# GpSimd makes the low parts of two of three weight chunks in the mixing stages of a two-block layer stack

## Chip, cores and metric

One core of one Trainium2 chip runs the whole program. The time is device microseconds of one execution; what is compared is the median of several runs. Three runs of the kernel before took 1978.05, 1983.33 and 1986.85 us.

## What is computed

The input is one sequence of 512 tokens of width 1024 and a context of 256 tokens. A first block of two layers (windowed attention, a Fourier mix, a short convolution, gated merge) gives x; a second block of two layers follows. A layer of the second block, cut to what matters here:

```python
def hybrid_layer(x, ...):
    proj = x @ w_in                                   # 1024 -> 2336
    o_a = dilated_mixture(...)                        # 6 heads
    o_b = rms_norm(diff_attention(...), subln_g)      # 4 heads, two softmaxes each
    q = rms_norm(c_q, q_norm_g) @ w_uq
    kv = rms_norm(c_kv, kv_norm_g) @ w_ukv
    o_c = causal_attention(...)                       # 6 heads
    h = layer_norm(ALPHA * x + concat(o_a, o_b, o_c) @ w_o, ...)
    ffn = (silu(h @ w_gate) * (h @ w_up)) @ w_down
    return layer_norm(ALPHA * h + ffn, ...)
```

All of it is float32, with a result close to float32 precision.

## The kernel before

**Split numbers.** Every matrix product is made of three TensorE products. A float32 operand is split into a high part (ScalarE writes a copy in TensorE's shorter float type, `hi`, L165) and a low part (VectorE subtracts the high part from the original, `lo`, L169, or L171 with a scale). `mm3` (L212 to L214) then adds high by high, high by low and low by high in one PSUM bank. A weight chunk goes through `w` (from L178): SyncE's queue loads it into a raw tile `wr` (3 buffers), ScalarE writes `wh`, VectorE writes `wl` from `wr` and `wh`, both of which lie in SBUF. There are 5 buffers each of `wh` and `wl`, and 2 more that a chunk takes when its running number modulo 7 is 2 or 5. A full chunk is 128 partitions by 1024 elements; 299 chunks pass through `w`.

**A layer of the second block** is a mixing stage (`second_mix`) and an output stage (`second_out`: w_o, the gated feed-forward product, two layer norms). A mixing stage uses 22 chunks: four of 128x832 for the latent projection (`proj_nat`, token tile by token tile), fifteen of 128x1024 for `proj_t` (three for each of five units of the kinds A and B), two of 128x768 for w_uq and one for w_ukv. There are eight units of two heads each, in the order B, C, B, C, A, C, A, A. A unit's projections are written ahead of the attention of the unit before it, and the attention stands at a higher priority; a list scheduler of the tile framework sets the order on each engine from dependencies, priorities and its own estimates. That order is fixed when the program is built, and each engine takes its instructions strictly one after another.

**Unit B** (`differential`): the projection lies in PSUM, and for each of four tiles ScalarE writes the high part (L165) and VectorE the low part (L171 for queries, L169 for keys), in turn; then GpSimd copies the high part to a third place (L1163, `qk<-qk`), and only then can the scores (L1025, `sps<-qk`) be made. Attention itself (`att2`): VectorE adds the bias table and takes the minimum (L1028), ScalarE takes the exponential (L1032), TensorE turns tiles (L1058), ScalarE and VectorE split them (`pth`, `ptl`), TensorE multiplies by V (L1074, L1075).

**GpSimd's queue before** holds: the reciprocal root of every norm (`rstd`: `rv` L219, `rr` L222), the loads of the bias tables (L950, which wait for a table's buffer), the copies L1163 and L1135, the zeroing L1133 and L1160, and loads and stores of activations (L897, L907, L1343). At the seam of the two blocks the last norm of the first block runs for token tiles 0 to 3: `rv` and `rr` on GpSimd, the scaling of x on VectorE (L905, two instructions a tile), a store (L907), then TensorE's transposes `tps<-ident,x` (L410), which feed the latent projection.

Of the kernel before, what the change touches and what calls it, by code (L numbers as in the profile page):

```python
# [9 lines left out]
F32 = mybir.dt.float32  # L10
F32R = mybir.dt.float32r
AF = mybir.ActivationFunctionType
ALU = mybir.AluOpType
# [27 lines left out]
def _host_constants():  # L41
# [27 lines left out]
    def dft(n):  # L69
        k = np.arange(n)  # L70
        w = 2.0 * np.pi * ((k[:, None] * k[None, :]) % n) / n
        return np.cos(w) / math.sqrt(n), np.sin(w) / math.sqrt(n)
# [45 lines left out]
class _Kernel:  # L118
    def __init__(self, es, tc, A, out):
        self.tc, self.nc, self.A, self.out = tc, tc.nc, A, out  # L120
        E = es.enter_context
        self.wx, self.wi = None, 0
        self.cst = E(tc.tile_pool(name="cst", bufs=1))
        self.sm = E(tc.tile_pool(name="sm", bufs=8))
        self.wp = E(tc.tile_pool(name="wp", bufs=5))
        self.xp = E(tc.tile_pool(name="xp", bufs=1))
        self.ps = E(tc.tile_pool(name="ps", bufs=1, space=PSUM))
        self.dr = E(tc.tile_pool(name="dr", bufs=1, space=DRAM))
        self.fp_es = ExitStack()
        self.fp = self.fp_es.enter_context(tc.tile_pool(name="fp", bufs=1, reuse_waits="tile"))  # L130
# [48 lines left out]
    def w(self, shape, parts, post=None):  # L179

        raw = self.wp.tile([P] + shape, F32, tag="wr", bufs=3, name="wr")
        for dst, src in parts:
            self.nc.sync.dma_start(raw if dst is None else dst(raw), src)
        if post is not None:
            post(raw)
        self.wi += 1
        if self.wx is not None and self.wi % 7 in (2, 5):
            pool, x, n = self.wx, "x", 2
        else:
            pool, x, n = self.wp, "", 5  # L190
        h = pool.tile([P] + shape, F32R, tag="wh" + x, bufs=n, name="wh")
        l = pool.tile([P] + shape, F32R, tag="wl" + x, bufs=n, name="wl")
        self.split(h, l, raw)
        return h, l

    def wblock(self, src, c0, n=P):
# [758 lines left out]
    def second(self):  # L955
        tc, nc, A = self.tc, self.nc, self.A
        with ExitStack() as es:
            self.sp = es.enter_context(tc.tile_pool(name="sp", bufs=1, reuse_waits="tile"))
            self.wx = self.sp
            self.rope2 = self.sp.tile([P, SEQ], F32, name="rope2")  # L960
            nc.gpsimd.dma_start(self.rope2, A["rope2"])
            self.ropek = self.sp.tile([P, NX, 64], F32, name="ropek")
            nc.gpsimd.dma_start(self.ropek, A["ropek"])
            self.half2 = self.sp.tile([P, 2], F32, name="half2")
            nc.gpsimd.memset(self.half2, 0.0)
            nc.gpsimd.memset(self.half2[0:64, 0:1], 1.0)
            nc.gpsimd.memset(self.half2[64:128, 1:2], 1.0)
            for l in range(DEPTH):
                with tc.tile_pool(name="a2", bufs=2, reuse_waits="tile") as pool:
                    heads = self.second_mix(l, pool)  # L970
                with tc.tile_pool(name="o2", bufs=2, reuse_waits="tile") as pool:
                    self.second_out(l, pool, heads)

# [357 lines left out]
    def second_out(self, l, pool, heads):  # L1331
# [71 lines left out]
        for gi, nf in enumerate(groups):  # L1403
# [20 lines left out]
            def down(t, c, w):  # L1424
                tok = slice(t * P, (t + 1) * P)
                ps = self.acc(c.stop - c.start)
                self.mm3(ps, [(Hs[k][0][:, tok], Hs[k][1][:, tok]) + w(k) for k in range(nf)])
                h = H[t]
                nc.vector.scalar_tensor_tensor(  # L1429
                    h[:, c], h[:, c], ALPHA if gi == 0 else 1.0, ps, op0=ALU.mult, op1=ALU.add  # L1430
                )
# [76 lines left out]
```

## Time and profile before

| what | value |
|---|---|
| median of 3 runs | 1983.33 us (1978.05 to 1986.85) |
| profiled execution | 1981.64 us |
| its span, first to last instruction | 1979.9 us |
| mean granted TensorE clock | 0.993 of 2.4 GHz |
| TensorE (PE) busy | 1901.3 us, 96% |
| VectorE (DVE) busy | 1203.6 us, 61% |
| ScalarE (ACT) busy | 894.1 us, 45% |
| GpSimd (POOL) busy | 169.7 us, 9% |

The profiled execution is 1.7 us below the median, and 1.7 us of it lie outside the span. Busy shares are means over stages; the rows below show them by stage. A line number such as L169 is that of the kernel before; where a helper does the work, all its uses have one line and the tile's name tells them apart.

### The profile page before, as it was taken

The page shows a single profiled execution, that of the slowest core. Times are in us where ns is not written, and L with a number is a line of the kernel's source. Part 1 is how long each engine was busy: PE and PEld are TensorE (multiplying, and loading weights), DVE is VectorE, ACT ScalarE, POOL GpSimd, SP SyncE. Part 2 cuts the span into 40 slices and gives each one's busy share as a digit, 9 for nine tenths or more (in the row PEclk, how much of TensorE's full clock was granted, in tenths as well). Part 3 has the DMA queues.
Part 4 walks back from the last instruction along what each step waited for, and adds up shares of the span by engine and source line. Part 5 has one row for each costly group of instructions (what it writes and reads, how often), then busy time and mean ns, then how long its engine had stood idle before and what let it go on. Part 6 is the DMA issues. An engine that isn't in the chain of part 4 may idle for free.

```text
span 1979.9 us, 25710 instructions
## 1 busy us (share of the span) xinstructions
PE 1901.3 (96%) x9564; PEld 1560.8 (79%) x9564; DVE 1203.6 (61%) x2350; ACT 894.1 (45%) x1744; POOL 169.7 (9%) x299
## 2 busy tenths in 40 slices
PE   6999999999999999899999999999999999999997
PEld 3878788778878777777888888887777788888886
DVE  3759984375988578776733434366876664243444
ACT  4736662384755558665221322215866432132220
POOL 2100000030000132101200000012211010000001
PEclk9999999999999999999999999999999999999999
DMA  8414342042332361223432324325122332232421
GB/s 291 148 54 140 96 128 85 23 160 79 118 87 63 111 167 43 65 86 111 119 96 85 107 75 117 94 80 130 41 64 95 124 107 96 75 117 64 128 75 43
DMA packets 220448, 197.19 MB, mean 100 GB/s; under 512 B 30154, under 2 KB 178128, under 8 KB 220324
## 3 DMA queue, kind: packets, MB, share of 16 engines
q1 hardware_dynamic: 209940, 160.32, 27.3%
q0 software_dynamic: 10384, 35.24, 5.2%
q8 instruction: 75, 1.23, 0.3%
q14 instruction: 49, 0.40, 0.1%
HBM read 187.09 MB, written 12.03 MB: 101 GB/s over the span
## 4 chain that ended last, share of the span: by engine, by line
PE 80%; ACT 6%; DVE 5%; issue 2%; DMA 1%; POOL 1%; POOLq 0%; DVEq 0%; ACTq 0%; SPq 0%
PE acc L212 22%; PE acc L213 22%; PE acc L214 22%; PE sps L1025 2%; PE tps L792 1%; PE tps L1058 1%; ACT wh L165 1%; PE pv L803 1%; PE pv L1074 1%; PE pv L804 1%; DVE wl L169 1%; PE pv L1075 1%; PE tps L410 1%; DMA wr<-in_w_mod_dram 1%; ACT L L1032 1%
## 5 line engine op out<-in xcount | busy, mean ns | idle before, releaser
L165 ACT ACTIVATE wh<-wr 128x1024 fp32r<-128x1024 f32 (+3 forms) x299 | 311.9, 1045 | 605.3 <-PE acc L213 262.5
L169 DVE TENSOR_TENSOR wl<-wr,wh 128x1024 fp32r<-128x1024 f32 (+3 forms) x299 | 358.3, 1202 | 259.2 <-ACT wh L165 256.5
L212 PE MATMUL acc<-xt,wh 128*128 128x512 f32 (+1 forms) x1200 | 465.9, 388 | 2.1 <-DVE kb L169 1.7
L214 PE MATMUL acc<-xt,wl 128*128 128x512 f32 (+1 forms) x1200 | 464.7, 387 | 0.0
L213 PE MATMUL acc<-xt,wh 128*128 128x512 f32 (+1 forms) x1200 | 463.7, 386 | 0.0
L212 PEld LDWEIGHTS acc<-xt,wh 128*128 128x128 f32 x1200 | 226.2, 188 | 41.5 <-DVE kb L169 2.4
L214 PEld LDWEIGHTS acc<-xt,wl 128*128 128x128 f32 x1200 | 226.1, 188 | 39.8
L213 PEld LDWEIGHTS acc<-xt,wh 128*128 128x128 f32 x1200 | 226.2, 188 | 39.2
L212 PE MATMUL acc<-wh,ht 128*128 128x512 f32 (+1 forms) x494 | 193.1, 391 | 1.3 <-ACT ht L165 1.1
L213 PE MATMUL acc<-wl,ht 128*128 128x512 f32 (+1 forms) x494 | 192.1, 389 | 0.0
L214 PE MATMUL acc<-wh,ht 128*128 128x512 f32 (+1 forms) x494 | 191.7, 388 | 0.0
L165 ACT ACTIVATE pth<-tps 128x384 fp32r<-128x384 f32 (+1 forms) x176 | 90.1, 536 | 90.4 <-PE tps L792 48.4
L169 DVE TENSOR_TENSOR ptl<-tps,pth 128x384 fp32r<-128x384 f32 (+1 forms) x176 | 104.7, 614 | 25.4 <-ACT pth L165 24.1
L212 PEld LDWEIGHTS acc<-wh,ht 128*128 128x128 f32 x494 | 92.9, 188 | 23.0 <-ACT ht L165 2.6
L214 PEld LDWEIGHTS acc<-wh,ht 128*128 128x128 f32 x494 | 93.0, 188 | 21.2 <-DVE ht L169 0.4
L213 PEld LDWEIGHTS acc<-wl,ht 128*128 128x128 f32 x494 | 92.9, 188 | 20.0
L1032 ACT ACTIVATE L<-L,nm 128x512 f32<-128x512 f32 (+3 forms) x160 | 89.0, 557 | 31.2 <-DVE nm L1028 29.8
L1429 DVE SCALAR_TENSOR_TENSOR h<-h,acc 128x512 f32<-128x512 f32 (+1 forms) x50 | 33.2, 665 | 114.9 <-PE acc L214 114.9
L1395 DVE SCALAR_TENSOR_TENSOR th<-th,acc 128x512 f32<-128x512 f32 x42 | 28.9, 688 | 113.3 <-PE acc L214 113.1
L1028 DVE CUSTOM_DVE_ANT_0 L<-sps,T 128x512 f32<-128x512 f32 (+3 forms) x160 | 75.4, 487 | 25.4 <-PE sps L1025 23.5
L219 POOL TENSOR_SCALAR rv<-bna 128x1 f32<-128x1 f32 x16 | 18.8, 1173 | 789.0 <-DVE bna L1324 789.0
L214 PE MATMUL acc<-wh,xt 128*128 128x256 f32 (+2 forms) x256 | 85.1, 333 | 1.0 <-DVE xt L169 0.8
(317 smaller groups left out, 3352.2 us busy)
## 6 DMA issues: line engine op xcount, KB each, us to landing
wr<-in_w_in_dram SPq DMA_DIRECT2D x66, 512.0 KB, 4.6
wr<-in_w_gate_dram SPq DMA_DIRECT2D x44, 512.0 KB, 3.8
wr<-in_w_up_dram SPq DMA_DIRECT2D x44, 512.0 KB, 3.9
wr<-in_w_down_dram SPq DMA_DIRECT2D x42, 512.0 KB, 3.5
wr<-in_w_mod_dram SPq DMA_DIRECT2D x40, 512.0 KB, 4.5
wr<-in_w_o_dram SPq DMA_DIRECT2D x32, 256.0 KB, 3.6
T<-skew POOLq DMA_DIRECT2D x26, 256.0 KB, 2.9
x<-in_x_dram POOLq DMA_DIRECT2D x8, 512.0 KB, 7.1
```

Of the source, the lines that this page charges most:

```text
L165: self.nc.scalar.activation(out, in_, AF.Copy, scale=scale)
L169: self.nc.vector.tensor_tensor(out, in_, hi.bitcast(F32), op=ALU.subtract)
L212: mm(ps, lh, rh, start=(first and i == 0), stop=False)
L213: mm(ps, lh, rl, start=False, stop=False)
L214: mm(ps, ll, rh, start=False, stop=(last and i == n - 1))
L410: nc.tensor.transpose(v[:, k, :], src[:, (kb * 4 + k) * P : (kb * 4 + k + 1) * P], self.ident)
L792: nc.tensor.transpose(tp[:, hq * P : (hq + 1) * P], Ps[hq][:, i * P : (i + 1) * P], self.ident)
L1025: nc.tensor.matmul(ps[:, :w], x[:, tok], y[:, :w], start=(k == 0), stop=(k == len(s) - 1))
L1028: nc.vector.tensor_tensor_reduce(lc, ps[:, :n], T[:, SEQ - n : SEQ], 1.0, 3.0e38, op0=ALU.add, op1=ALU.min, accum_out=nm[:, i : i + 1],)
L1032: nc.scalar.activation(lc, lc, AF.Exp, bias=nm[:, i : i + 1], scale=-1.0, accum_out=sums[:, i : i + 1])
L1395: nc.vector.scalar_tensor_tensor(th, th, 0.5, pu, op0=ALU.mult, op1=ALU.mult)
L1429: nc.vector.scalar_tensor_tensor(h[:, c], h[:, c], ALPHA if gi == 0 else 1.0, ps, op0=ALU.mult, op1=ALU.add)
```

## The change

A field `share` is 0, except while `second_mix` is written out, where it is 2. In `w`, a chunk whose running number modulo 3 is below `share` has its low part subtracted by GpSimd instead of VectorE; the high part stays on ScalarE.

```diff
         h = pool.tile([P] + shape, F32R, tag="wh" + x, bufs=n, name="wh")
         l = pool.tile([P] + shape, F32R, tag="wl" + x, bufs=n, name="wl")
-        self.split(h, l, raw)
+        self.hi(h, raw)
+        if self.wi % 3 < self.share:
+            self.nc.gpsimd.tensor_tensor(l, raw, h.bitcast(F32), op=ALU.subtract)
+        else:
+            self.lo(l, raw, h)
         return h, l
...
                 with tc.tile_pool(name="a2", bufs=2, reuse_waits="tile") as pool:
+                    self.share = 2
                     heads = self.second_mix(l, pool)
+                    self.share = 0
```

29 of the 44 chunks of the two stages move: 15 in the first (three of 128x832, ten of 128x1024, two of 128x768), 14 in the second (two, ten, two). The scheduler then sets a new order. Lines behind L193 are 6 higher in the changed kernel, and behind L970 8 higher.

**GpSimd, the seam of the blocks and the head of the first mixing stage.** `rv_7012` and `rr_7014` are the norm of token tile 3, the last of the first block. Before:

```order
L967 MEMSET half_7043 64x1
L907 DMA xs_6582<-x 128x1024
L219 TENSOR_SCALAR rv_7012<-ssum 128x1
L222 TENSOR_TENSOR rr_7014<-rv_7012,mhalf 128x1
L907 DMA xs_6582<-x 128x1024
L1100 DMA dl<-in_diff_lambda_dram 128x128
```

Now:

```order
L197 TENSOR_TENSOR wl<-wr,wh 128x832
L972 MEMSET half_7043 64x1
L973 MEMSET half_7043 64x1
L197 TENSOR_TENSOR wl<-wr,wh 128x832
L913 DMA xs_6582<-x 128x1024
L225 TENSOR_SCALAR rv_7012<-ssum 128x1
L228 TENSOR_TENSOR rr_7014<-rv_7012,mhalf 128x1
L197 TENSOR_TENSOR wl<-wr,wh 128x1024
L913 DMA xs_6582<-x 128x1024
L197 TENSOR_TENSOR wl<-wr,wh 128x1024
L1108 DMA dl<-in_diff_lambda_dram 128x128
```

Two low parts of 832 elements now stand ahead of the norm of tile 3, and two of 1024 behind it.

**GpSimd, the copies of the first unit B in the first mixing stage.** The eight copies are four for queries, then four for keys. Before:

```order
L222 TENSOR_TENSOR rr_7255<-rv_7253,mhalf 128x2
L1163 COPY qk<-qk 32x512 x2
L1160 MEMSET qk 32x512
L1163 COPY qk<-qk 32x512 x4
L1160 MEMSET qk 32x512
L1163 COPY qk<-qk 32x512 x2
L950 DMA T<-skew 128x512 x4
```

Now:

```order
L228 TENSOR_TENSOR rr_7255<-rv_7253,mhalf 128x2
L197 TENSOR_TENSOR wl<-wr,wh 128x1024
L1171 COPY qk<-qk 32x512 x2
L1168 MEMSET qk 32x512
L1171 COPY qk<-qk 32x512 x2
L197 TENSOR_TENSOR wl<-wr,wh 128x1024
L1171 COPY qk<-qk 32x512 x2
L1168 MEMSET qk 32x512
L1171 COPY qk<-qk 32x512 x2
L956 DMA T<-skew 128x512 x4
```

One low part stands ahead of the first query copy, another between the query copies and the key copies.

**TensorE, the first scores of that unit**, among the products of its V projection. Before:

```order
L213 MATMUL acc<-xt,wh 128x512
L214 MATMUL acc<-xt,wl 128x512
L212 MATMUL acc<-xt,wh 128x512
L1025 MATMUL sps<-qk 128x256
L213 MATMUL acc<-xt,wh 128x512
L214 MATMUL acc<-xt,wl 128x512
L212 MATMUL acc<-xt,wh 128x512
L213 MATMUL acc<-xt,wh 128x512
L214 MATMUL acc<-xt,wl 128x512
L1025 MATMUL sps<-qk 128x256
```

Now (the same stretch of the projection, from five products earlier):

```order
L219 MATMUL acc<-xt,wh 128x512
L1033 MATMUL sps<-qk 128x256
L220 MATMUL acc<-xt,wl 128x512
L218 MATMUL acc<-xt,wh 128x512
L219 MATMUL acc<-xt,wh 128x512
L220 MATMUL acc<-xt,wl 128x512
L218 MATMUL acc<-xt,wh 128x512
L1033 MATMUL sps<-qk 128x256
```

Both score products stand five products earlier than before.

## Rows read from the trace of the kernel before

**Rows 1.** Busy time by stage: microseconds, then PE, PEld, DVE, ACT, POOL, clock, DMA

```profile
702.00:913.00 211.00, 195.00 (x1013) 155.58 (x1012) 161.30 (x399) 143.19 (x345) 38.05 (x62) 0.99 0.28 79
915.00:1336.00 421.00, 420.51 (x1951) 348.65 (x1952) 193.94 (x237) 108.80 (x141) 19.73 (x25) 1.00 0.33 99
1340.00:1552.00 212.00, 195.96 (x1003) 155.66 (x1002) 159.24 (x397) 141.98 (x343) 37.13 (x60) 0.98 0.28 79
```

**Rows 2.** Waits of PE, 702 to 913 us: total us, times, longest us

```profile
PE acc L999 <- ACT vt L996: 4.1, 5, 1.4
PE tps L1118 <- DVE sq L1113: 2.4, 1, 2.4
PE sps L1025 <- DVE nm L1028: 1.5, 3, 0.6
PE tps L1058 <- DVE ptl L169: 1.4, 2, 1.3
PE acc L212 <- DVE V L1004: 1.0, 1, 1.0
PE pv L1074 <- DVE heads L1085: 0.9, 1, 0.9
PE tps L1272 <- DVE ct L171: 0.9, 1, 0.9
```

**Rows 3.** Low parts of weights on DVE, 702 to 853 us: ns min/median/max, shapes

```profile
L169 DVE TENSOR_TENSOR wl<-wr,wh x17: 947/1218/1226, 703.0 to 851.6; 128x1024 fp32r<-128x1024 f32 x14, 128x768 fp32r<-128x768 f32 x3
```

**Rows 4.** DVE in time: start us, us, what [idle before, releaser]

```profile
693.25 1.95 DVE L169 TENSOR_TENSOR wl<-wr,wh 128x832 fp32r<-128x832 f32 x2
696.99 1.41 DVE L905 SCALAR_TENSOR_TENSOR x<-y,rr,x 128x512 f32<-128x512 f32 x2
698.31 1.22 DVE L169 TENSOR_TENSOR wl<-wr,wh 128x1024 fp32r<-128x1024 f32 x1
...
721.09 1.23 DVE L169 TENSOR_TENSOR wl<-wr,wh 128x1024 fp32r<-128x1024 f32 x1 [0.80 <-ACT wh L165]
...
726.30 1.23 DVE L169 TENSOR_TENSOR wl<-wr,wh 128x1024 fp32r<-128x1024 f32 x1 [0.59 <-ACT wh L165]
```

**Rows 5.** POOL in time: tiny norms, copies, a table load

```profile
692.43 0.12 POOL L965 MEMSET half<- 128x2 f32 x1
...
695.45 0.19 POOL L219 TENSOR_SCALAR rv<-ssum 128x1 f32<-128x1 f32 x1 [1.27 <-DVE ssum L901]
...
721.68 1.11 POOL L1163 CAST qk<-qk 32x512 fp32r<-32x512 f32 x1 [5.43 <-ACT qk L165]
723.72 0.60 POOL L1163 CAST qk<-qk 32x512 fp32r<-32x512 f32 x1 [0.93 <-ACT qk L165]
...
759.28 0.79 POOL L1163 CAST qk<-qk 32x512 fp32r<-32x512 f32 x1 [3.48 <-ACT qk L165]
...
833.13 0.20 POOL L219 TENSOR_SCALAR rv<-ssb 128x8 f32<-128x8 f32 x1 [3.13 <-DVE ssb L1184]
```

**Rows 6.** PE in time: transposes at the seam, two first uses, scores, two waits

```profile
697.84 0.63 PE L410 MATMUL tps<-ident,x 128*128 128x128 f32 x4
...
698.93 0.44 PE L213 MATMUL acc<-wl,xt 128*128 128x416 f32 x1
...
714.67 0.39 PE L214 MATMUL acc<-xt,wl 128*128 128x512 f32 x1
...
729.11 0.36 PE L1025 MATMUL sps<-qk 96*128 96x256 f32 x1
...
733.66 0.66 PE L999 MATMUL acc<-ident,vt 128*128 128x128 f32 x4 [1.27 <-ACT vt L996]
735.20 1.31 PE L1272 MATMUL tps<-ident,xs 128*128 128x128 f32 x8 [0.89 <-DVE ct L171]
```

**Rows 7.** Costliest POOL arithmetic of 700 to 915 us, shapes apart: busy us, mean ns

```profile
L222 POOL TENSOR_TENSOR rr<-rv,mhalf 128x8 f32<-128x8 f32 x2 | 3.3, 1668 | 0.2
```

**Rows 8.** Busy time and clock around one group of waits in the second mixing stage

```profile
1368.00:1392.00 24.00, 19.87 (x89) 14.54 (x88) 18.89 (x51) 17.28 (x44) 2.90 (x5) 0.86 0.20 56
```

More of the change, by code (lines that the diff above doesn't have):

```diff
@@ L969, in second @@
                 with tc.tile_pool(name="a2", bufs=2, reuse_waits="tile") as pool:
+                    self.share = 2
                     heads = self.second_mix(l, pool)
+                    self.share = 0
                 with tc.tile_pool(name="o2", bufs=2, reuse_waits="tile") as pool:
```

## The prediction

> **What bounds the kernel now.** I read the busy time by stage first [rows 1]. In the output stage between the mixing stages TensorE is busy for 420.5 of 421 us: nothing on another engine can shorten it, and the change leaves it alone. The two mixing stages are different: TensorE is busy for 195.0 of 211 us and for 196.0 of 212 us, so 16 us stand idle in each, 32 us in all, or 1.6% of the time. That is the most that any relief of VectorE can bring. VectorE is the next busiest there (161 and 159 us, three quarters), GpSimd the least (38 and 37 us, under a fifth). The list of waits then says who ends TensorE's idle time [rows 2]: the six largest rows that name VectorE make 8.1 us, the one that names ScalarE (`vt`) 4.1 us. None names a weight's low part, so no product waits for weights; what a low part can do is stand ahead of something else on VectorE.
>
> That weights are early is seen from a low part and its first use: the one made at 698.31 [rows 4] is first read by TensorE at 714.67 [rows 6], 15 us after its end. It is the first of the fifteen full chunks, with the shortest lead of them, as the later ones are made up to seven buffers ahead. Only the 832 wide chunks at the seam are closer: the pair that ends at 695.2 [rows 4] is first read until 698.93 [rows 6], under 4 us later.
>
> **What leaves VectorE.** The median full low part takes 1.22 us and the 768 wide one 0.95 us [rows 3]; two of 832 take 1.95 us together [rows 4]. The 29 that move are 20 x 1.22 + 4 x 0.95 + 5 x 0.98 = 33.1 us, about 16.5 us in each stage, a tenth of VectorE's work there.
>
> **What arrives on GpSimd.** The trace has no large two-input subtraction on GpSimd. The nearest row is a copy of 512 elements at 0.60 us [rows 5], 1.2 ns an element with one input. From below, two inputs cost no more than one: 1.2 us for 1024. From above, twice the price of reading both in turn: 4.8 us. I take the middle, both inputs read in turn, 2.4 us for 1024, 1.95 us for 832. The `rr` row would give far more (1.67 us for 8 elements [rows 7]), but that one raises to a power; the copy is a plain pass like the subtraction, so I hold it nearest. By the Trainium skill (GPSIMD Engine Reference, section 3.1) a tensor-tensor addition of 2048 elements takes 4.5 us, so an estimate of 2.25 us for 1024; the sum would move by some tenths. At 2.4 us the 29 take 20 x 2.4 + 4 x 1.8 + 5 x 1.95 = 65 us, and GpSimd's busy time rises from 38 to some 71 of 211 us: still no bound as an engine. What counts is the queue, as each low part waits for its high part and everything behind it waits too.
>
> **Place one, the seam, a loss.** Tile 3's norm starts on GpSimd at 695.45, after 1.27 us of idle time [rows 5]. The scaling on VectorE (696.99) follows and, with no time to spare, TensorE's transposes at 697.84 [rows 4, 6], between products that are ready. Now two 832 wide low parts stand ahead of that norm. The first can begin when the memset of 692.43 is over, near 692.6, and VectorE's work on tile 2 may hold it to 693.3. Two times 1.95 us end near 697.2; still ahead of their products (698.93); with the store behind them the norm starts 1.9 us late or a little more. VectorE has lost the same two low parts and is waiting then, so the 1.9 us reach the transposes whole: **+1.9 us**. Other products are ready by then, but TensorE takes its queue in order and stands at the transposes. In the second mixing stage the new order has the 832 wide parts a tile earlier, behind the store of tile 2: nothing, or at worst 1.9 us again.
>
> **Place two, the first unit B, a gain.** The eight splits run in turn over ScalarE and VectorE; low parts at 721.09 and 726.30 [rows 4] each delay that chain by up to 1.2 us, and behind it stand `vt` (wait 1.27 us at 733.66) and `ct` (0.89 us at 735.20) [rows 6]. In the first stage both of those low parts move, and the next one, beside `ct`, stays. Against that, the copy of the first key tile now stands behind a low part which cannot start before its high part (VectorE waited for that one until 726.30 [rows 4]; I add 0.3 us, as ScalarE now makes a fourth query split ahead of it) and ends near 729.0; the copy follows until 729.6. The scores that need it stood at 729.11 and are now five products earlier, near 728.0: a new wait of about 1.5 us where 0.5 us was. But TensorE waits behind this for `vt` and `ct` anyway, so the group ends when their chain does. The chain is 2.4 us shorter and gets some of that back as `vt` now follows the next chunk's high part; I take **-0.7 us** for the group in the first stage. In the second stage the low part beside `ct` moves too and no low part stands between the copies: **-1.8 us**. There the clock is 0.86 over 24 us [rows 8], that is part of the time at the lower level, after the same group of waits; in the first stage it is not. What this costs, 24 x 0.14 = 3.4 us, may come back or may befall the first stage; I count neither and keep it for the range.
>
> **Everything else.** Some 6 us of VectorE-ended waits remain in each stage; a tenth less work there is worth 0.6 us a stage. I set this against VectorE being held up by GpSimd's reads (below) and count zero. Lateness of low parts I cost at nothing: the 15 us above cover a low part of 2.4 us that waits behind a table load. If one took 15 us more, the products themselves would wait next.
>
> **Sum:** 1.9 - 0.7 - 1.8 = -0.6 us against the profiled 1981.64 us, which is 1.7 us below the median of the runs shown. As a median I expect 1983.33 - 0.6 = **1982.7 us**: no change. Runs of one kernel spread over 0.45%, so 0.5%, 9.9 us, is about what a measurement can tell here.
>
> **Rival one: the queue costs more than it gives (slower).** A low part takes 4.8 us instead of 2.4. Each place where a short GpSimd step stands closely behind one then overruns its idle time: the seam by 2 x 2.0 = 3.9 us more; the first key copy by 2.4 us more; the second root of `ssb` (idle 3.13 us before it [rows 5], with a low part in that gap in the new order, in both stages) by 1.7 us each; the copy at 759.28 (idle 3.48 us [rows 5]) by 1.3 us, and its like in the second stage: 3.9 + 2.4 + 3.4 + 2.6 = 12.3 us, so **1995 us**. It begins to decide above some 3 us a low part, where those gaps are full. For it: no row shows the price. Against: the copy's 0.60 us. Chance 0.19.
>
> **Rival two: the engines hold each other (no change, a little slower).** The trace shows one direction: the copy at 721.68 takes 1.11 us instead of 0.60, beside VectorE's low part from 721.09 to 722.32, and ends 0.47 us after it [rows 4, 5]: it stood until VectorE was through. If GpSimd coming first holds VectorE in the same way, then VectorE's instructions with two SBUF inputs meet them: the seven low parts that stay in a stage, 8.5 us, and by the code about twice as many others (the mixes of L in unit B, the query splits of unit C). GpSimd's low parts fill 33 us of 211, so some 3 to 4 of these 21 a stage wait, 1.2 us on average: 4 us of the 16.5 us gained. If all of that reached TensorE and none of the relief did, +8 us, **1991 us** at most; I put this case at 1986. The Trainium skill (SBUF, State Buffer; Who interferes with whom) says that a VectorE instruction with two SBUF inputs and a GpSimd one that reads SBUF exclude each other, and the first to issue holds the second for its whole length. The trace agrees for the one direction; no row here has the other. Chance 0.20.
>
> **Rival three: VectorE was the cause of more (faster).** If half of the 12.2 us of waits in each stage go [rows 2] and the 3.4 us of clock return, it is 12.2 + 3.4 = 15.6 us: **1967.7 us**. Against: TensorE's waits name results of VectorE that wait for TensorE or ScalarE themselves. Chance 0.12.
>
> That the change does nothing at all is excluded: the new order has the 29 on GpSimd.
>
> **How the numbers follow.** The forecast has 0.49. Faster by over 0.5%: 0.10 from rival three and 0.02 from the forecast's own spread, 0.12. Slower by over 0.5%: 0.14 from rival one, 0.05 from rival two, 0.19. Within: 0.69. The range leaves out most of rival three and the upper part of rival one: 1973 to 1996 us.
>
> **What would show it.** Right: some 2.4 us for a low part on GpSimd, VectorE's busy time down by some 33 us, a new wait near 1.9 us of the transposes L410 at the seam, smaller waits for `vt` and `ct`, no wait of a product for `wl`. Wrong: low parts over 3 us, or waits for `wl`, for the copies or for `rr` that sum to more than 10 us; or idle time in the mixing stages below 25 us in all.

## The result: 2006.5 us, slower by 1.16%, and the profile after

| | before | after |
|---|---|---|
| median of 4 runs | 1983.51 us (1978.05 to 1986.85) | 2006.52 us (2003.79 to 2008.52) |
| ratio, 95% interval | | 1.0116 (1.0100 to 1.0133) |
| profiled execution | 1981.64 us | 2004.88 us |
| mean granted clock of that execution | 0.993 | 0.987 |

The prediction was 1982.7 us, in a range from 1973 to 1996, with no change the likeliest: the time lies 10 us outside the range, on the slow side. The median of before has one run more than ahead of the prediction. All four runs of after have a mean clock of 0.985 to 0.987; of nineteen runs of before the median is 0.993.

**The totals.** The head of the page of the kernel after (span, then busy time, share and count of each engine):

```profile
span 2003.1 us, 25723 instructions
PE 1912.9 (95%) x9564; PEld 1568.2 (78%) x9564; DVE 1190.2 (59%) x2321; ACT 894.8 (45%) x1744; POOL 232.8 (12%) x328
```

The span is 23.2 us longer. TensorE does the same 9564 matmuls, but is busy for 11.6 us more (before 1901.3), and the other 11.6 us are idle time (90.2 us instead of 78.6). The first half is the clock: 0.993 - 0.987 = 0.006 of 1980 us is 12 us. VectorE's busy time fell by only 13.4 us, where 33.1 us of work left it (29.7 us less busy where the low parts are left out, experiment 1); GpSimd's rose by 63.

**By stage**, as [rows 1] for before (microseconds, then PE, PEld, DVE, ACT, POOL, clock, DMA):

```profile
702.00:920.00 218.00, 199.50 (x1012) 158.96 (x1010) 152.22 (x383) 141.19 (x338) 64.67 (x76) 0.97 0.28 79
920.00:1344.00 424.00, 421.79 (x1962) 348.12 (x1961) 192.04 (x237) 110.78 (x148) 23.06 (x26) 1.00 0.31 96
1348.00:1568.00 220.00, 200.25 (x997) 159.99 (x995) 152.71 (x382) 141.51 (x338) 65.51 (x76) 0.95 0.27 79
```

The output stage is untouched. The loss is at the seam ahead of the first window (690 to 702 us) and in the mixing stages, whose clock reads 0.97 and 0.95 instead of 0.99 and 0.98. Followed matmul by matmul, after lies 4.3 us behind before once the seam is over, 11.6 us after 770 us, 12.6 us at the end of the first mixing stage and all through the output stage, and 23.2 us at the end of the second.

**TensorE's waits**, as [rows 2] (total us, times, longest us): 690 to 920 us, then 1330 to 1565 us.

```profile
PE acc L1007 <- ACT vt L1004: 3.7, 5, 1.4
PE sps L1033 <- POOL qk L1171: 3.2, 2, 2.8
PE tps L1066 <- DVE L L1056: 1.9, 2, 1.7
PE tps L416 <- DVE ssum L907: 1.8, 1, 1.8
...
PE tps L1126 <- DVE sq L1121: 1.4, 1, 1.4
PE tps L416 <- issue: 1.3, 1, 1.3
...
PE acc L218 <- DVE kb L171: 2.5, 2, 2.2
...
PE sps L1033 <- DVE qk L171: 2.2, 2, 1.2
...
PE tps L1066 <- DVE L L1056: 1.9, 2, 1.7
PE acc L218 <- DVE kt L1268: 1.7, 1, 1.7
```

New are the transposes at the seam (L416, 1.8 + 1.3 us; the releaser named `ssum` is the next thing on VectorE behind the scaling of x), the first scores that wait for GpSimd's copies (3.2 us), and in each stage the transposes of L, that wait for VectorE's mix of L (1.9 us). These make 3.1 + 3.2 + 2 x 1.9 = 10.1 us, most of the 11.6 us of new idle time. A fourth new wait, 1.7 us at the head of the second stage (`kt`), has a cause of its own, which experiment 6 follows. Other rows grew (`kb` and `qk` in the second stage) or shrank (`vt`, `sq`) beside these. No row names `wl`: the low parts are in time.

**The low parts on GpSimd** cost what was forecast (its costliest groups, 690 to 920 us: busy us, mean ns):

```profile
L197 POOL TENSOR_TENSOR wl<-wr,wh 128x1024 fp32r<-128x1024 f32 x10 | 24.9, 2492 | 30.5 <-ACT wh L167 13.9 <-PE tps L1066 13.2 <-PE acc L220 3.2
L197 POOL TENSOR_TENSOR wl<-wr,wh 128x832 fp32r<-128x832 f32 x2 | 4.1, 2040 | 0.1
```

and in time (start, us), as [rows 5]:

```profile
692.61 1.99 POOL L197 TENSOR_TENSOR wl<-wr,wh 128x832 fp32r<-128x832 f32 x1
694.87 2.09 POOL L197 TENSOR_TENSOR wl<-wr,wh 128x832 fp32r<-128x832 f32 x1
698.47 0.18 POOL L225 TENSOR_SCALAR rv<-ssum 128x1 f32<-128x1 f32 x1
...
731.89 2.34 POOL L197 TENSOR_TENSOR wl<-wr,wh 128x1024 fp32r<-128x1024 f32 x1
734.30 1.27 POOL L1171 CAST qk<-qk 32x512 fp32r<-32x512 f32 x2
...
766.43 2.37 POOL L197 TENSOR_TENSOR wl<-wr,wh 128x1024 fp32r<-128x1024 f32 x1 [1.53 <-ACT wh L167]
```

**VectorE beside them** (in time, start and us, as [rows 4]):

```profile
692.04 5.46 DVE L911 SCALAR_TENSOR_TENSOR x<-y,rr,x 128x512 f32<-128x512 f32 x2 [0.57 <-POOL rr L228]
...
766.18 4.44 DVE L1056 SCALAR_TENSOR_TENSOR L<-L,sum 128x128 f32<-128x128 f32 x4
...
857.91 1.97 DVE L1121 COPY iv<-inv 128x512 f32<-128x512 f32 x1
```

The statistics of line L1056, the mix of L (ns least/median/most; who waited for it, us and times):

```profile
L1056 DVE SCALAR_TENSOR_TENSOR L<-L,sum x32: 341/611/2653, 755.1 to 1459.7; 128x128 f32<-128x128 f32 x8, 128x256 f32<-128x256 f32 x8, 128x384 f32<-128x384 f32 x8, 128x512 f32<-128x512 f32 x8
...
  PE tps L1066: 3.8, 4
```

This is where the time is made. Two scalings of x took 1.41 us before [rows 4] and take 5.46 us now: the pair runs from 692.04 to 697.50, beside the two low parts of 692.61 and 694.87, and it ends half a microsecond after the second low part does. The mix of L (L1048 before) was never above 747 ns and nobody waited for it:

```profile
L1048 DVE SCALAR_TENSOR_TENSOR L<-L,sum x32: 341/545/747, 747.5 to 1438.1; 128x128 f32<-128x128 f32 x8, 128x256 f32<-128x256 f32 x8, 128x384 f32<-128x384 f32 x8, 128x512 f32<-128x512 f32 x8
```

Now one 256 wide piece of it in each stage takes 2.65 us instead of 0.48, beside a low part of 2.37 us. Of all VectorE instructions of 650 to 1600 us, twelve take over 0.3 us longer than is usual for their line and shape, two of them the next pieces of L, beside a copy of GpSimd; together they are 16.1 us longer. In the trace of before none is. Nearly all read two operands from SBUF; one, `iv<-inv`, is a copy from SBUF to SBUF (usual 0.42 us). The splits of unit B that begin beside a low part (726.60, 727.94, 732.32 and 733.66 us) read one of their operands from PSUM, and keep their usual 0.68 us.

**The clock** (windows of the two traces, columns as above; of after first, then of before):

```profile
690.00:710.00 20.00, 16.97 (x86) 15.40 (x85) 12.72 (x14) 8.95 (x18) 14.84 (x19) 0.91 0.72 204
730.00:745.00 15.00, 10.37 (x47) 7.56 (x45) 7.49 (x11) 8.57 (x13) 7.89 (x11) 0.89 0.38 102
1385.00:1400.00 15.00, 11.72 (x36) 8.08 (x36) 7.50 (x21) 9.22 (x22) 3.46 (x3) 0.66 0.24 70
```

```profile
690.00:710.00 20.00, 19.87 (x108) 18.44 (x107) 14.58 (x30) 9.37 (x22) 7.59 (x18) 1.00 0.81 229
730.00:745.00 15.00, 11.11 (x56) 7.69 (x54) 11.45 (x27) 12.07 (x27) 3.55 (x6) 1.00 0.30 87
1365.00:1385.00 20.00, 15.41 (x63) 10.73 (x62) 13.97 (x34) 14.19 (x32) 4.65 (x8) 0.83 0.28 79
```

Each 0.1 below 1.00 means a fifth of the stretch at 1.2 instead of 2.4 GHz. The third row of each is the same group of waits in the second stage, some 16 us later in the trace of after. In that trace the level falls at 696.9 us, in the second wait at the seam, and rises again at 700.3 us; it falls anew at 734.5 us, behind the wait for the key copies. Before, both places ran at 1.00. From 650 to 1600 us the lower level fills 13.7 us before and 41.0 us after: 27.3 us more, up to half of which, 13.7 us, is lost work. One execution is not enough for the size of this: the traces of four runs that cost nothing have 13.7 (fills), 15.0 (second B), 23.0 (late units) and 23.9 us (low parts left out) at the lower level there, so some 10 of the 27.3 us lie within what executions differ by. The mean clock of all four runs of after does lie below that of each of the nineteen runs of before (0.985 to 0.987 against 0.990 to 0.995).

### The profile page after: what moved, and what is told of

The parts are those of the page before. It is cut to its first block, busy times and chain, and to the rows that moved or that the text cites. A ratio compares the mean times of both kernels' runs of the same rounds, so it can differ in the third digit from the quotient of the medians.

```text
span 2003.1 us, 25723 instructions
## 1 busy us (share of the span) xinstructions
PE 1912.9 (95%) x9564; PEld 1568.2 (78%) x9564; DVE 1190.2 (59%) x2321; ACT 894.8 (45%) x1744; POOL 232.8 (12%) x328
## 5 line engine op out<-in xcount | busy, mean ns | idle before, releaser
L171 DVE TENSOR_TENSOR wl<-wr,wh 128x1024 fp32r<-128x1024 f32 (+3 forms) x270 | 327.3, 1214 | 259.4 <-ACT wh L167 254.7
L1040 ACT ACTIVATE L<-L,nm 128x384 f32<-128x384 f32 (+3 forms) x160 | 89.1, 558 | 34.9 <-DVE nm L1036 34.0
L1036 DVE CUSTOM_DVE_ANT_0 L<-sps,T 128x384 f32<-128x384 f32 (+3 forms) x160 | 75.6, 487 | 32.3 <-PE sps L1033 27.8
```

Of the source, the lines that this page charges most:

```text
L171: self.nc.vector.tensor_tensor(out, in_, hi.bitcast(F32), op=ALU.subtract)
L1036: nc.vector.tensor_tensor_reduce(lc, ps[:, :n], T[:, SEQ - n : SEQ], 1.0, 3.0e38, op0=ALU.add, op1=ALU.min, accum_out=nm[:, i : i + 1],)
L1040: nc.scalar.activation(lc, lc, AF.Exp, bias=nm[:, i : i + 1], scale=-1.0, accum_out=sums[:, i : i + 1])
```

## Experiments

Three explanations were to be told apart. **The lock (theory one):** a GpSimd instruction that reads SBUF, once begun, holds VectorE's instructions with two SBUF inputs to its end, and some of those are what TensorE waits for next. **The queue (theory two):** GpSimd's short steps (norms, key copies) stand behind low parts, and that alone is the loss. **The clock** would come behind either, or with the new order by itself. Each kernel ran beside the kernel before. Busy and idle are TensorE's in the profiled execution, as differences to before (1901.3 and 78.6 us); it is one execution, up to 4.2 us off the median of its run, and that of before lies 1.9 us under its median. The medians of before beside the runs were 1983.5 to 1985.1 us; an excess named below is against the one beside its run.

| run | median us | ratio, 95% interval | busy | idle |
|---|---|---|---|---|
| the change | 2006.52 | 1.0116 (1.0100 to 1.0133) | +11.6 | +11.6 |
| low parts left out | 1985.58 | 1.0004 (0.9994 to 1.0014) | +4.9 | -0.8 |
| extra subtraction | 2009.78 | 1.0126 (1.0105 to 1.0147) | +12.7 | +19.6 |
| extra fills | 1986.81 | 1.0006 (0.9996 to 1.0016) | 0.0 | +6.7 |
| extra copies | 1995.62 | 1.0050 (1.0033 to 1.0066) | +8.4 | +9.6 |
| low parts in pieces | 2000.42 | 1.0069 (1.0054 to 1.0084) | +8.4 | +11.0 |
| without the seam | 2002.71 | 1.0094 (1.0072 to 1.0115) | +8.3 | +12.2 |
| late units only | 1985.75 | 1.0001 (0.9987 to 1.0016) | +4.1 | +1.7 |
| second B and first A | 1997.11 | 1.0054 (1.0032 to 1.0076) | +6.3 | +9.1 |
| first A only | 1994.68 | 1.0050 (1.0035 to 1.0065) | +6.8 | +5.8 |
| second B only | 1984.49 | 1.0006 (0.9994 to 1.0017) | +0.9 | +0.3 |
| seam only | 1987.39 | 1.0017 (1.0008 to 1.0027) | +2.8 | +2.9 |
| without seam and first A | 1994.22 | 1.0048 (1.0031 to 1.0065) | +7.5 | +8.1 |
| without these and second B | 1992.74 | 1.0036 (1.0021 to 1.0052) | +10.8 | +3.3 |

**1. Is the relief of VectorE worth anything?** The moved chunks get no low part at all.

```diff
         if self.wi % 3 < self.share:
-            self.nc.gpsimd.tensor_tensor(l, raw, h.bitcast(F32), op=ALU.subtract)
-        else:
-            self.lo(l, raw, h)
+            return h, h
+        self.lo(l, raw, h)
```

> The 29 chunks have no low part at all: TensorE reads their high part in its place, so part of the products is left out and GpSimd does nothing new. Lock theory (GpSimd's subtraction, once begun, holds VectorE's instructions with two SBUF inputs) and queue theory (steps on GpSimd come late behind a low part) both expect the relief alone: 1977 to 1984 us, no time at the seam and no lengthened VectorE instruction. Order theory (the new fixed order of the engines costs the time by itself) expects 1990 us or more.

Ratio 1.0004 (1985.58 us, a little above both forecasts' 1977 to 1984): 29 low parts, 33.1 us of VectorE's work, can vanish from VectorE and from GpSimd, and the time stays. So the change had nothing to win. Two reservations: the mean clock of these runs is 0.991 at the median where that of before is 0.993, some 4 us of busy time, so a few us of idle time may be saved and given back by the clock; and TensorE's order here is a new one, different from that of the change in 1001 of 9564 places, so it shows that such a new order can cost nothing, not what the order of the change costs (experiment 4 does, for the seam).

**2. GpSimd reads, or only writes.** VectorE makes all low parts as before; for the same 29 chunks GpSimd then does something superfluous with the raw tile: one subtraction (2.39 us), two fills (0.96 us each), or two copies (1.04 and 1.14 us).

```diff
+        self.lo(l, raw, h)
         if self.wi % 3 < self.share:
-            self.nc.gpsimd.tensor_tensor(l, raw, h.bitcast(F32), op=ALU.subtract)
-        else:
-            self.lo(l, raw, h)
+            self.nc.gpsimd.tensor_tensor(raw, raw, h.bitcast(F32), op=ALU.subtract)
```

> VectorE makes all low parts as before; GpSimd makes 29 extra subtractions of the same size, each into the raw tile once its low part is done, so nothing reads them. Lock theory: 1993 to 2005 us, with VectorE instructions of over twice their usual length beside GpSimd's. Queue theory: the same total, but without lengthened VectorE instructions; waits for copies and roots instead. Order theory: whatever it is, near the next run (fills).

The fills have, in place of the last line, twice

```diff
+            self.nc.gpsimd.memset(raw, 0.0)
```

> As the run with extra subtractions, but GpSimd fills the raw tile twice instead (about the same 2.4 us, SBUF written and not read). Lock theory (only a reading GpSimd instruction excludes VectorE): 1983 to 1988 us, no lengthened VectorE instruction. Queue theory: within 4 us of the run with extra subtractions.

and the copies twice

```diff
+            self.nc.gpsimd.tensor_copy(raw, h.bitcast(F32))
```

> As the run with extra subtractions, but GpSimd copies the high part into the raw tile twice: one input from SBUF instead of two, about the same 2.4 us in all. If any GpSimd instruction that reads SBUF holds VectorE's two-input instructions: 1993 to 2008 us, VectorE instructions lengthened by up to 1.2 us each. If it takes two inputs on GpSimd: 1984 to 1989 us like the fills, none lengthened.

GpSimd's groups (690 to 920 us) of the run with the subtraction:

```profile
L198 POOL TENSOR_TENSOR wr<-wr,wh 128x1024 f32<-128x1024 f32 x10 | 23.9, 2385 | 37.4 <-ACT L L1039 17.0 <-ACT pth L167 14.0 <-DVE wl L171 3.7
```

One VectorE row of it in time, and GpSimd's row beside it:

```profile
698.81 1.96 DVE L906 TENSOR_TENSOR ssum<-ss 128x1 f32<-128x1 f32 x1
...
698.10 2.65 POOL L198 TENSOR_TENSOR wr<-wr,wh 128x832 f32<-128x832 f32 x1 [0.24 <-DVE wl L171]
```

GpSimd's groups of the run with the fills:

```profile
L198 POOL MEMSET wr<- 128x1024 f32 x10 | 9.6, 956 | 29.3 <-DVE inv L1049 13.9 <-DVE wl L171 12.1 <-issue 3.0
L199 POOL MEMSET wr<- 128x1024 f32 x10 | 9.5, 954 | 0.5
```

GpSimd's busy time in the fills' run is 218.6 us, near the 232.8 of the change, and they cost 0.06%, which is within the noise. No VectorE instruction is lengthened. The subtraction, with 240.0 us, costs 1.26% (2009.78 us, above the lock theory's 1993 to 2005), though VectorE lost no work and no product waits for it; VectorE's instructions are lengthened by 19.2 us, down to an addition of 128x1 that takes 1.96 us instead of 0.15 and ends 20 ns after GpSimd does. So it is the reading, not the time in the queue. The copies read one operand and hold VectorE too, for about 1 us at a time (8.8 us of lengthening), and cost 0.5%. That is the shape of the lock; a load of GpSimd as such is excluded, and so is, at this size, a raw tile that is merely kept longer, as the fills keep it too.

**3. Shorter instructions on GpSimd.**

```diff
-            self.nc.gpsimd.tensor_tensor(l, raw, h.bitcast(F32), op=ALU.subtract)
+            n = shape[0]
+            for a in range(0, n, max(1, n // 4)):
+                c = slice(a, a + max(1, n // 4))
+                self.nc.gpsimd.tensor_tensor(l[:, c, :], raw[:, c, :], h[:, c, :].bitcast(F32), op=ALU.subtract)
```

> As the change, but a low part of 1024 elements is made by GpSimd in four instructions of 256, the others in pieces of 384 to 416 or 128. Lock theory: VectorE is held for one piece only, at most some 0.7 us instead of 2.4, so the lengthened part of VectorE falls from 16 us to under 7 and the time to 1988 to 1998 us. Queue theory (GpSimd's total time ahead of copies and roots counts): as the change or slower, 2004 to 2012 us.

Pieces of 256 elements take 0.8 us each, 3.2 us for a full chunk. The lengthening halves (8.8 us), and the loss falls from 23 to 16 us, between the two forecasts. The queue is longer in exchange: the scores wait 4.0 us for the copies. Both terms exist.

**4. The seam taken away, and alone.**

```diff
-        if self.wi % 3 < self.share:
+        if self.wi % 3 < self.share and shape[1] != 416:
```

> As the change, but the 832 wide chunks at the head of a mixing stage stay on VectorE; TensorE's order is the same as in the change. Lock and queue theory: the 4.3 us at the seam of the first stage go, the rest stays: 2000 to 2003 us. Order theory: 2006 us, unchanged.

With `== 416` in place of `!= 416`:

> GpSimd makes the low parts of the 832 wide chunks alone, five of them in both stages, all others stay on VectorE. The change with these left out was 4 us faster than the whole change. Theory one: the scaling of x at the seam is held, 2.4 to 3.1 us instead of 0.75, and TensorE's transposes start about 4 us late; with the lower clock behind it 4 to 6 us, near 1990. Theory two (the norm of tile 3 stands behind the low parts in the queue, and nothing more): the 1.9 us of the prediction, near 1987.

Left out, the seam gives 3.8 us back (2006.52 to 2002.71); alone it costs 3.4 us. TensorE's order is that of the change in the first run and that of the kernel before in the second, product for product, so the order is no part of this difference. The seam alone, VectorE and TensorE in time:

```profile
692.31 5.46 DVE L911 SCALAR_TENSOR_TENSOR x<-y,rr,x 128x512 f32<-128x512 f32 x2 [0.46 <-POOL rr L228]
...
697.92 1.09 PE L416 MATMUL tps<-ident,x 128*128 128x128 f32 x4 [1.77 <-DVE ssum L907]
```

The same 5.46 us as in the whole change, and TensorE's matmuls behind it lie 4.2 us later (0.4 us at 690 us, 4.6 at 696): 2.9 us of waits for the two scalings of token tile 2, the rest the lower clock that begins in the second of them (697.3 us). The transposes of tile 3, whose norm the queue delays, add nothing. That is the lock's shift, not the queue's 1.9 us. As a whole run it costs less, as part of that comes back in the second stage; by the time alone, 1987.39 us, it would be the queue's 1987, and only the trace tells the two apart.

**5. Which units.** The field `share` is set for some units' projections alone (in the loop over the units, not in the layer's call):

```diff
+                self.share = 2 if i + 1 >= 6 else 0
                 nxt = proj(i + 1)
+                self.share = 0
```

> Only chunks of the last two units (A, A) are moved, two of three, 8 of the 29; no mixes of unit B and no seam beside them. Lock theory: within 4 us of the kernel before, 1983 to 1989 us, as few two-input VectorE instructions lie there. A cost per moved chunk (0.8 us each) expects 1991 us.

With `i + 1 in (2, 4)`, the second B and the first A:

> Only chunks of the second unit B and the first unit A are moved, 8 of the 29: their low parts fall beside the splits of unit B and its mixes. Lock and queue theory: most of the rest that the seam leaves, 1992 to 2000 us, with the copy's wait and the lengthened mix in both stages. A cost per moved chunk expects 1991 us too, but then as much in the run with the late units.

With `(4,)` and with `(2,)`, each alone:

> GpSimd makes the low parts of two of three chunks of one unit only, the first unit A, four chunks in both stages. Theory one (a GpSimd instruction that reads SBUF holds VectorE's instructions with two SBUF inputs): the mix of L, 2.6 us instead of 0.48 in each stage, comes from this unit, and TensorE's transposes wait for it; some 4 us of lengthening, with the lower clock behind it some 6 us in all, near 1991. Theory two (the loss is the queue of GpSimd, in which the key copies stand behind a low part): no copy of a unit B stands behind these low parts, so nothing, within 2 us of the kernel before.

> The same for the second unit B only, four chunks in both stages: the other half of the run with both units. Theory one: no instruction of VectorE on the path lies beside these, lengthening under 1.5 us, within 3 us of the kernel before. Theory two: the scores wait for the copies by 2 to 3 us a stage, which makes 5 to 7 us with the lower clock, near 1991. The two runs together should give the 12.5 us of the run with both units if the parts add up.

The last two are the clearest pair of the study: four low parts each, of the same 2.4 us. Those of the first A cost 0.50%, those of the second B nothing that can be measured. GpSimd, VectorE and TensorE in time in the run with the first A alone:

```profile
760.85 2.36 POOL L197 TENSOR_TENSOR wl<-wr,wh 128x1024 fp32r<-128x1024 f32 x1 [1.54 <-ACT wh L167]
...
760.57 4.47 DVE L1054 SCALAR_TENSOR_TENSOR L<-L,sum 128x128 f32<-128x128 f32 x4
...
763.55 0.44 PE L1064 MATMUL tps<-ident,L 128*128 128x128 f32 x2 [1.67 <-DVE L L1054]
```

and in the run with the second B alone:

```profile
727.85 2.37 POOL L197 TENSOR_TENSOR wl<-wr,wh 128x1024 fp32r<-128x1024 f32 x1
730.28 1.26 POOL L1169 CAST qk<-qk 32x512 fp32r<-32x512 f32 x2
...
730.94 0.38 PE L1031 MATMUL sps<-qk 96*128 96x256 f32 x1 [1.99 <-POOL qk L1169]
```

In the first, a low part that begins beside the mix of L adds 2.3 us to TensorE's way in each stage, 4.6 us. The median is 10.7 us up, more than the 6 us that I expected; the mean clock of its four runs is 0.988 to 0.990, where the median of before is 0.993, which makes 6 to 10 us with the same matmuls. Part of that is not shown to come from the held piece: in the profiled execution the level also falls at 738.5 us, ahead of the first of these low parts, which makes 2.6 us. In the second, the key copies do stand behind a low part and TensorE does wait 2.0 us for them; but its matmuls behind that group lie only 1.2 us later, as it had waited there for `vt` and `ct` anyway, and the mean clock of the execution is that of before, 0.993. A wait of that size is not yet a loss. The two add up: 10.7 + 0.5 = 11.2 us, against 12.5 us together. Eight low parts of the last two A units cost nothing: they hold two instructions of VectorE (`iv`, 1.96 us, and a piece of L, 2.85 us), but nobody waits for that piece, and the wait for `iv` (0.9 us instead of 0.2) comes with one for `sq` that is 0.3 us shorter.

**6. Do the two costly places explain the whole?** The change without the seam's chunks (as in 4) and without those of the first A:

```diff
+                self.share = 0 if i + 1 == 4 else 2
                 nxt = proj(i + 1)
+                self.share = 2
```

> The whole change without its two costly places: the 832 wide chunks of the seam and the chunks of the first unit A stay on VectorE, twenty low parts stay on GpSimd. Theory one (the loss is made where a GpSimd low part holds a VectorE instruction that TensorE is about to wait for; these two places cost 3.4 and 10.7 us alone): what is left is some 23.0 - 14.1 = 9 us at most, near 1993, with the mix of L back at 0.5 us; if the parts that are left have no held instruction on the path, nothing is left, 1985. Theory two (the load on GpSimd as a whole, 48 us of low parts still, slows VectorE everywhere): most of the loss stays, over 2000.

and with `in (2, 4)`, without the second B's too:

> The run without the two costly places, and the chunks of the second unit B on VectorE too: no low part stands ahead of or between the copies of the first unit B any more, sixteen low parts stay on GpSimd. If the 10 us that remained are the queue's (the scores wait 4.6 us for the key copies, and the clock is lower behind it), nothing or little is left: within 3 us of the kernel before, 1984 to 1987, with no wait for the copies over 1 us. If they are those of the VectorE instructions that are still held (xs, the 768 wide low part, the norm of h), most stays: 1991 to 1995.

Without both, 1994.2 us: 10.0 us above the kernel before beside it, so 13.0 of the 23.0 us are gone, where 14.1 were expected, although twenty of 29 low parts are still there. The parts add up; the load on GpSimd as such is not it. The 10 us that remain are not the key copies' either: with no low part near the copies, only 1.5 us less, within the spread of the two runs, and in the range (1991 to 1995) that the instructions still held were to give. TensorE's first scores in that last run, in time:

```profile
733.74 0.36 PE L1033 MATMUL sps<-qk 96*128 96x256 f32 x1 [2.56 <-DVE qk L171]
```

and its windows from 730 us (columns as above):

```profile
730.00:745.00 15.00, 10.50 (x39) 7.13 (x37) 9.87 (x13) 8.40 (x13) 6.03 (x9) 0.75 0.37 101
745.00:760.00 15.00, 13.08 (x52) 10.16 (x52) 11.09 (x38) 10.24 (x28) 0.54 (x1) 0.79 0.11 37
```

Here VectorE has two low parts of its own right ahead of the splits and one among them (730.93 us), the scores wait for a split instead of a copy, and 30 us at 0.75 and 0.79 follow, up to 7 us of work lost, where before ran at 1.00. Its idle time is only 3.3 us up, its busy time 10.8 (this execution took 3 us more than the run's median). The clock of one execution proves little here, though: the run with the late units alone, as fast as before, reads 0.76 and 0.90 in the same two windows.

Why the splits come late can be read from the traces. A load of a weight chunk needs one of the three raw tiles, and a raw tile comes free when the low part made from it is done. SyncE (705 to 730 us; a row is a group of loads, with the start of the first) and ScalarE in this run, then before:

```profile
718.27 9.26 SPq L185 DMA_DIRECT2D wr<-in_w_in_dram  x5
722.95 1.06 ACT L167 ACTIVATE wh<-wr 128x1024 fp32r<-128x1024 f32 x1 [5.61 <-DMA wr<-in_w_in_dram]
```

```profile
713.57 14.36 SPq L183 DMA_DIRECT2D wr<-in_w_in_dram  x6
717.97 1.06 ACT L165 ACTIVATE wh<-wr 128x1024 fp32r<-128x1024 f32 x1 [2.78 <-DMA wr<-in_w_in_dram]
```

TensorE lies 2.2 us behind before at this place, but the load starts 4.7 us later, when VectorE's low part of a 768 wide chunk is through. That low part begins late (716.55 us), and it is itself held, 1.69 us instead of 0.95, beside GpSimd's low part of 715.54. ScalarE waits 5.61 us for the load, and the splits of unit B stand behind it on ScalarE; TensorE's 2.56 us follow. Likewise at the head of the second stage: a load waits for a low part on GpSimd (1345.66 to 1348.56 us), ScalarE waits 5.17 us for the load, and TensorE 2.1 us for `kt`. In the whole change the same load waits for GpSimd's low part until 1351.50 us, ScalarE waits 4.13 us for it, and TensorE the 1.7 us. In the runs with a single unit the 768 wide low parts are on VectorE, and the load is on time (714.69 us with the second B alone, TensorE 1.1 us behind before). So these two waits, 4.7 us, and the clock behind them are what this trace shows of the rest. It is a third path: a low part that is late, by the lock or by the queue, keeps a raw tile, the tile keeps a load waiting, and the load keeps ScalarE. No run was made with more raw tiles, so its share in the 23 us is not shown by an experiment. No kernel of these was faster than the kernel before.

## Why the prediction was wrong, by its own steps

- **What bounds the kernel: right.** The output stage is as it was, and no product waits for a low part.
- **The low part on GpSimd, 2.4 us: right.** 2.49 us on the mean in the first stage, 2.04 us for 832. The Trainium skill's figure (GPSIMD Engine Reference, section 3.1), from which I had worked out an estimate of 2.25 us, is close.
- **33.1 us leave VectorE: wrong in effect.** Its busy time fell by 13.4 us: 29.7 us less, as in experiment 1, and 16.1 us back as lengthening. And the relief, whole as in experiment 1, shortens nothing.
- **Place one, +1.9 us: mis-sized, 4.3 us, and by another way.** I saw the norm of tile 3 behind two low parts. It began 3.0 us late (698.47, before 695.45 [rows 5]), as VectorE's scaling of tile 2 was held by the same two low parts, and on GpSimd the store of that tile stands ahead of the norm. But TensorE waits for that scaling of tile 2 itself (1.3 and 1.8 us), a place that I had not seen, and no longer for tile 3, whose transposes start without a wait (702.22). The lower clock is the rest of the 4.3 us. In the second stage the transposes wait for nothing, as said.
- **Place two, -0.7 and -1.8 us: the first wrong in the change, the second near.** The key copies start at 734.30, right behind the low part of 731.89; the scores wait 2.8 us where I had 1.5, and TensorE is 4 us later before some 0.7 us come back. With the second B's chunks alone the group made about +1.2 and -1.4 us, and the run the time of before. In the second stage of the change TensorE does gain 1.0 us over that group, where I had 1.8, and loses it again behind it, by a wait of 1.4 us for `nm` and the lower clock.
- **"Everything else", counted at zero: the step that failed.** It set 1.2 us of relief against VectorE being held by GpSimd's reads. The relief is nothing, and the holding is 16.1 us on VectorE, 10.1 us of new waits on TensorE (3.2 us of them the queue's), and the clock behind them.
- **Lateness of low parts, "at nothing": wrong at one place in the change.** I asked only whether products wait for a low part. A late low part also keeps its raw tile, and with it the next load and ScalarE: 1.7 us of wait for `kt` in the second stage, and more in the runs of experiment 6.
- **The clock, "I count neither": the second failure.** In the two profiled executions it is half of the loss. I had 3.4 us of it in view at one place [rows 8] and took it for a matter of chance between stages; with the new waits came new stretches at 1.2 GHz, in all 11.6 us of busy time in the profiled execution, part of which may be such chance.

**The rivals.** The third (faster) falls with experiment 1. The first rested on low parts of 4.8 us, which they are not; its mechanism, a short step behind a low part, is there at the copies, with the smaller price; at the seam the norm of tile 3 is late too, but no wait of TensorE comes of it. The second was the mechanism, with the wrong price: 8 us at most. I counted chance meetings, 3 to 4 a stage at 1.2 us, 8 us in all; twelve came to 16.1 us, twice that. What I missed above all is *where*: I counted low parts, L and query splits as a pool of equal instructions, without asking for each on whose way it lies. Two scalings at the seam and one piece of L in each stage alone make 8.4 us of lengthening, and TensorE was standing behind each. The Trainium skill's rule (SBUF, State Buffer; Who interferes with whom), that the first to issue holds the other for its whole length, now has its second direction in a trace: 2.65 us for a piece of 0.48 beside a low part of 2.37. By the recorded starts it is not always the later one that is held: the first scaling at the seam starts 0.57 us ahead of the low part (692.04 and 692.61), and is held all the same. The Trainium skill's sentence that an instruction that only writes does not contend is borne out by the fills, at 0.06%. Held against [rows 4], it would have put the scalings at the seam into the sum; I cited it and then let an average decide.

## What to carry to other kernels

Work moved from VectorE to an idle GpSimd is not free even where GpSimd's queue is empty: list which VectorE instructions with two SBUF inputs can begin beside it, and ask for each whether the bound engine stands behind it; those count most, and each for the whole length of the GpSimd instruction. Ask too what a late result keeps from coming free, here a raw tile and with it the next load. Before relieving an engine at all, ask what its relief is worth: leaving the work out in one run answers it. And where TensorE is the bound, a new wait can cost more than its own length when the clock falls behind it: about as much again in the change, nothing in the run with the fills (6.7 us more idle, 0.0 more busy), so it has to be looked up for each trace.

## What had not been expected of the hardware

Size is no protection: an addition of 128x1 (usual 0.15 us) was held to 1.96 us, one of 128x64 (0.22) to 1.87. A GpSimd copy, with one SBUF input, holds VectorE as a subtraction does, and a VectorE copy from SBUF to SBUF is held too (1.97 us, usual 0.42). The holding goes both ways: in the trace of after, low parts on GpSimd took 3.46 us at 701.35 and 2.94 us at 1348.55, where 2.4 is usual, each beside an instruction of VectorE with two SBUF operands, which kept its usual time. Two GpSimd fills of a full chunk take 1.91 us together and hold nobody.
